# An encoder step on one core: one pool per tile at two changes of stage, the last block and the first up pairs in another order, and a convolution issued behind its own pair's split

## The chip, the core and the metric

One core of a Trainium2 chip runs the whole program. Its engines are TensorE (PE, matrix products), VectorE (DVE), ScalarE (ACT), GpSimd (POOL), and SyncE (SP), which issues most DMAs. Each takes its own instructions in a fixed order; they meet at semaphores. The time is device microseconds of one execution.

## The reference

The kernel computes one layer of a streaming encoder on 1024 prompt tokens and 8 x 16 sample tokens, 1152 tokens in all, with D_MODEL = 1024 and D_FF = 3072:

```
h = rmsnorm(x, g_pre_mix)
qa, ka, va, qb, kb, vb, ga, gb = split(h @ w_in)
oa = band_attention(qa, ka, va, window of 2 chunks, sinks)   # 8 heads, 2 kv heads
ob = band_attention(qb, kb, vb, band of 8 chunks)            # 8 heads
merged = sigmoid(ga) * (oa @ w_oa) + sigmoid(gb) * (ob @ w_ob)
x = x + rmsnorm(merged @ w_out, g_post_mix)
u, g = split(rmsnorm(x, g_pre_ffn) @ w_upg)
c = conv_b + sum over 3 taps of conv_w[tap] * shifted u
y = x + rmsnorm((gelu(c) * g) @ w_down, g_post_ffn)
```

All inputs and outputs are float32; new keys, values and convolution rows are outputs too.

## The kernel before, in words

A float32 product is made of three matrix products: each operand is split into a high part (a cast on ScalarE) and a low part (operand minus high part, on VectorE or GpSimd), and high x high, high x low and low x high are summed in PSUM. So each weight or activation tile costs a ScalarE and a VectorE instruction ahead of its matmuls. The large products (the projections, up, down) use seven block products in place of eight; their sums of blocks are further VectorE work.

The stages are: the projections; **attention** (units 0 to 7, each with sub-bands 0 to 3: scores `s` on PE, bias and maximum on VectorE, exponentials `p` at L701 on ScalarE, reciprocal and normalisation at L714 and L718 on VectorE, transpositions `pt` at L735 on PE, copies `pk` at L737 and L739, values `o`, store to `o_dr` at L753); into its gaps the dense columns of the gates are laid (`d`, L117 to L119, evicted as `gt` at L570); **merge** (L920 to L1000): `outputs` loads the eight attention outputs oT0 to oT7 (L931), casts (L932) and subtracts (L933); class `Rows` makes a row block of 128 of merged^T: `start` loads the gate and takes its sigmoid (L945), `part` multiplies (mp, L956 to L958), `gated` multiplies by the gate and so empties PSUM (mm, L962), `merge` adds the two branches (L967) and splits the sum into mT; **third** (L1015 to L1120): wt0 to wt7, the tiles of w_out, are loaded and split (`split_w`, L101 and L104); for each of nine blocks of 128 tokens the row product r (L1090 to L1092), Square (L1098), norm and residual (L1100, L1101), second norm (L1105), and a transposition `tp` (L1074) into the four quarters bq (L1080), from which the right factors b11, b21, t3, ... of the up stage are split; **up** (L1126 to L1300): 24 tiles f of the hidden width, each with u and gate; **down** (L1309 on).

In the up stage the first five tiles (NH = 5) have two of their products made ahead (`head_away`): xh<f> from b11, stored to a_dr, and after b21 is added, stored to c_dr. Later `head_back` and `up_rows` load these again (`a`, and `w`, the row buffer). For each f `tail` then makes the products with t3, t2, t1, b22, t4, and `take` (L1200) adds the product x and the loaded a on VectorE, which also frees the PSUM banks of x. `conv` works on the rows w: one tap on ScalarE (L1239), two on VectorE (L1241), then GELU.

Order: a scheduler lays every engine's instructions in a fixed order by priorities that come from the order of the code, and by costs that it assumes. `issue_after(i)` keeps instructions behind i, `high_priority(offset)` moves them ahead. Tiles live in pools of SBUF or PSUM space; a pool opened where an earlier one was closed waits until the instructions that used that space are done (by tile, with reuse_waits="tile"). In the kernel before, the eight oT tiles lie in one pool (op), and the eight wt tiles in one pool (wp3).

## Time and profile before

| what | value |
|---|---|
| time, median of 3 runs | 1635.86 us (1635.2 to 1637.76) |
| the profiled execution | 1635.94 us, its span 1634.1 us |
| PE busy | 1593.4 us, 98% of the span |
| VectorE busy | 1099.4 us, 67% |
| ScalarE busy | 728.7 us, 45% |
| GpSimd busy | 212.1 us, 13% |
| chain that ended last | PE 86%, DVE 5%, ACT 3%, DMA 3% |

How to read it: the busy share of PE counts a matmul that runs at the lower level of the clock with its longer time, so a stretch can be full and slow at once. The granted clock of the whole execution is 0.994. The idle time in front of an instruction is given in brackets, with the instruction that ended it.

### The profile page before, as it was taken

What the parts mean: (1) busy time and instruction counts of PE and PEld (TensorE: products, weight loads), DVE (VectorE), ACT (ScalarE), POOL (GpSimd) and SP (SyncE); (2) the same over time, 40 slices, a digit from 0 to 9 for tenths busy, and PEclk for the clock granted to TensorE, in tenths of its full rate; (3) what the DMA queues carried; (4) which work ended last, traced back from release to release, by engine and by line L of the source; (5) the groups of instructions that cost most, each with busy time, mean ns of one, the idle gap of its engine ahead of it and who ended that gap; (6) DMA issues with size and microseconds to landing.
All of it is one profiled execution on the core that took longest, in us unless ns stands there. A gap on an engine that the chain in (4) does not pass through costs nothing.

```text
span 1634.1 us, 27922 instructions
## 1 busy us (share of the span) xinstructions
PE 1593.4 (98%) x10891; PEld 1470.7 (90%) x10891; DVE 1099.4 (67%) x2045; ACT 728.7 (45%) x1429; POOL 212.1 (13%) x287
## 2 busy tenths in 40 slices
PE   8999999999999999999999999999999999999998
PEld 6999999878788889978899999999999998888886
DVE  6976544777676746444497866766666767955997
ACT  7521233566555444332374344444444445434252
POOL 1000000221110004410002212211112211000002
PEclk9999999999999999999999999999999999999999
DMA  7654321654443255342264321221221219053023
GB/s 282 205 183 150 111 103 67 222 174 152 152 157 102 67 184 195 119 161 90 78 189 136 117 80 57 82 81 67 82 69 67 81 49 367 1 204 124 1 78 154
DMA packets 93045, 205.94 MB, mean 126 GB/s; under 512 B 19321, under 2 KB 42793, under 8 KB 92914
## 3 DMA queue, kind: packets, MB, share of 16 engines
q1 hardware_dynamic: 92640, 203.35, 36.2%
q8 instruction: 85, 1.39, 0.4%
q0 software_dynamic: 272, 0.81, 0.1%
q14 instruction: 46, 0.38, 0.1%
q10 hardware_dynamic: 2, 0.00, 0.0%
HBM read 147.61 MB, written 61.24 MB: 128 GB/s over the span
## 4 chain that ended last, share of the span: by engine, by line
PE 86%; DVE 5%; ACT 3%; DMA 3%; issue 2%; POOL 1%; SPq 0%; DVEq 0%; POOLq 0%; ACTq 0%
PE x L143 16%; PE z L143 8%; PE x L1415 8%; PE ix L143 7%; PE p L1415 6%; PE iz L143 4%; PE y L143 4%; PE o L750 2%; PE d L117 2%; PE pt L735 2%; PE d L119 2%; PE r L1090 2%; PE mp L956 2%; PE mp L958 2%; PE mp L957 2%; PE d L118 2%
## 5 line engine op out<-in xcount | busy, mean ns | idle before, releaser
L143 PE MATMUL x<-xot,s 128*128 128x288 f32 x1152 | 157.7, 295 | 1.5 <-DVE w L1200 1.5
L143 PEld LDWEIGHTS x<-xot,s 128*128 128x128 f32 x1152 | 154.9, 188 | 1.7 <-ACT a L1049 1.7
L1415 PE MATMUL x<-wbp,zap 128*128 128x512 f32 x576 | 135.3, 389 | 0.0
L1415 PEld LDWEIGHTS x<-wbp,zap 128*128 128x128 f32 x576 | 108.1, 188 | 22.5
L1049 ACT ACTIVATE s<-uw 128x512 fp32r<-128x512 f32 x96 | 60.2, 627 | 94.8 <-issue 41.7
L1415 PE MATMUL p<-wbp,zap 128*128 128x512 f32 x432 | 100.5, 389 | 0.0
L701 ACT ACTIVATE p<-p,m 128x256 f32<-128x256 f32 (+4 forms) x128 | 74.8, 587 | 57.3 <-DVE m L696 57.2
L1415 PEld LDWEIGHTS p<-wbp,zap 128*128 128x128 f32 x432 | 81.1, 188 | 16.9
L1050 DVE TENSOR_TENSOR s<-uw,s 128x512 fp32r<-128x512 f32 x96 | 70.2, 731 | 33.8 <-ACT s L1049 33.7
L1241 DVE SCALAR_TENSOR_TENSOR wk<-w,cw,wk 128x128 f32<-128x128 f32 (+2 forms) x144 | 83.2, 614 | 6.7 <-ACT wk L1239 5.9
L1050 DVE TENSOR_TENSOR a<-uw,a 128x512 fp32r<-128x512 f32 x62 | 42.9, 693 | 63.4 <-ACT a L1049 62.2
L143 PE MATMUL x<-xob,s 128*128 128x288 f32 x576 | 81.1, 295 | 3.3 <-DVE wk L1200 3.3
L143 PEld LDWEIGHTS x<-xob,s 128*128 128x128 f32 x576 | 78.1, 188 | 3.9 <-ACT wk L1239 3.1
L143 PE MATMUL z<-xot,s 128*128 128x288 f32 x576 | 80.7, 295 | 0.0
L143 PE MATMUL z<-xot,a 128*128 128x288 f32 x576 | 80.7, 295 | 0.0
L143 PE MATMUL ix<-t,s_i 128*128 128x256 f32 (+1 forms) x576 | 78.4, 294 | 0.7 <-DVE iu L191 0.7
L143 PEld LDWEIGHTS z<-xot,s 128*128 128x128 f32 x576 | 78.1, 188 | 0.0
L143 PEld LDWEIGHTS z<-xot,a 128*128 128x128 f32 x576 | 78.1, 188 | 0.0
L143 PEld LDWEIGHTS ix<-t,s_i 128*128 128x128 f32 x576 | 76.8, 187 | 0.9 <-DVE iu L191 0.9
L176 ACT ACTIVATE s_i<-iw 128x512 fp32r<-128x512 f32 x48 | 30.1, 631 | 86.2 <-PE ix L143 38.1
L143 PE MATMUL x<-xob,a 128*128 128x288 f32 x456 | 63.9, 295 | 0.0
L143 PE MATMUL y<-xob,a 128*128 128x288 f32 x456 | 63.9, 295 | 0.0
(634 smaller groups left out, 3837.1 us busy)
## 6 DMA issues: line engine op xcount, KB each, us to landing
uw<-in_w_upg SPq DMA_DIRECT2D x53, 512.0 KB, 3.7
iw<-in_w_in SPq DMA_DIRECT2D x24, 512.0 KB, 3.7
gg<-in_dr SPq DMA_DIRECT2D x16, 576.0 KB, 4.1
z_dr<-wk SPq DMA_DIRECT2D x23, 256.0 KB, 2.1
in_dr<-gt SPq DMA_DIRECT2D x30, 192.0 KB, 1.9
z_dr<-wk SPq DMA_DIRECT2D x23, 224.0 KB, 1.9
xt<-in_x SPq DMA_DIRECT2D x9, 512.0 KB, 7.6
oT<-o_dr SPq DMA_DIRECT2D x8, 576.0 KB, 6.5
```

The costliest lines, as they stand in the source:

```text
L117: nc.tensor.matmul(ps, w[:, 0, a], xg[0][:, b], start=start and k == 0, stop=False)
L118: nc.tensor.matmul(ps, w[:, 0, a], xg[1][:, b], start=False, stop=False)
L119: nc.tensor.matmul(ps, w[:, 1, a], xg[0][:, b], start=False, stop=stop and k == nk - 1)
L143: nc.tensor.matmul(ps, w[:, i, k], right(j, c, k), start=first and n == 0, stop=last and n == len(todo) - 1, skip_group_check=True)
L701: nc.scalar.activation(p[h][:, 0:n], p[h][:, 0:n], AF.Exp, bias=least[h], scale=-1.0, accum_out=st.d[:, h, i:i + 1])
L735: nc.tensor.transpose(pt[:, h * nb + b], st.p[i][h][:, c:c + P], ident[:])
L750: nc.tensor.matmul(ps[r, c], k.vs[:, kb, r], p[h], start=n == 0, stop=n == len(st.pv) - 1)
L956: nc.tensor.matmul(ps[:], self.sp[:, 0, k], oT[k][:, 0, c], start=k % 4 == 0, stop=False)
L1049: nc.scalar.activation(sp[:, 0], src, AF.Copy)
L1050: nc.vector.tensor_tensor(sp[:, 1], src, fr(sp[:, 0]), op=ALU.subtract)
L1241: nc.vector.scalar_tensor_tensor(out, src(t), cw[:, f, t:t + 1], out, op0=ALU.mult, op1=ALU.add)
L1415: nc.tensor.matmul(ps, z[:, i, k, c], w[:, j, k], start=first and n == 0, stop=last and n == 2, skip_group_check=True)
```

## The change

- **End of attention.** The last dense pieces come from one stream, four, then the transpositions, two, then the values, then the rest. The last eviction gt moves from ScalarE to VectorE, and the tile vs has a pool of its own.
- **Merge.** Eight pools in place of one for oT. The load and splits of oT2 to oT7, of the second row's weights and of the gates are issued behind the cast of oT1. The parts k come in pairs.
- **Third.** A pool per wt tile, the row buffers placed behind the fourth; the splits of wt have a higher priority (200).
- **Last block.** The transpositions of the two blocks before the last stand within the last block's product (k = 1 and 6). The last block's own normed rows lie in the unused end of two bq tiles, in two halves, and are transposed in the up stage.
- **Up.** Two weight tiles of the away pairs share a load buffer; three single pools for the split left factors, by turns. `Away` in place of `head_away`: the pairs 0, 1, 2 go by turns, first the b11 products of all three, then the last block's transpositions, then the b21 products; then pairs 3 and 4. `conv(0)` of these five pairs is issued behind the cast of the split that was made last, which is the pair's own s1; the right factors still to be made (`form`) are issued behind the last away split.

```diff
-        run(pieces[0])
+        rest = stream(pieces)
+        for _ in zip(range(4), rest):
+            pass
         for _ in transposes(prev):
             pass
-        run(pieces[1])
+        for _ in zip(range(2), rest):
+            pass
         values(prev)
-        run(*pieces[2:])
+        for _ in rest:
+            pass
...
-        op = ph.enter_context(tc.tile_pool(name="op", bufs=1, reuse_waits="tile"))
+        op = [ph.enter_context(tc.tile_pool(name=f"op{u}", bufs=1, reuse_waits="tile")) for u in range(8)]
...
-        oT = [op.tile([P, 2, T], F32R, name=f"oT{u}") for u in range(8)]
+        oT = [op[u].tile([P, 2, T], F32R, name=f"oT{u}") for u in range(8)]
...
-                nc.scalar.activation(oT[u][:, 0], raw, AF.Copy)
+                cast = nc.scalar.activation(oT[u][:, 0], raw, AF.Copy)
                 nc.vector.tensor_tensor(oT[u][:, 1], raw, fr(oT[u][:, 0]), op=ALU.subtract)
+            return cast
 
...
-        first = [Rows(n) for n in range(2)]
-        outputs(range(4))
-        for r in first:
-            r.start(0)
-        outputs(range(4, 8))
-        for k in range(4):
+        first = [Rows(0)]
+        cast = outputs(range(2))
+        with tc.issue_after(cast.ins):
+            first.append(Rows(1))
+            outputs(range(2, 4))
+            for r in first:
+                r.start(0)
+            outputs(range(4, 8))
+        for k in range(0, 4, 2):
             for r in first:
                 for g in groups:
-                    r.part(0, g, k)
+                    for i in range(2):
+                        r.part(0, g, k + i)
...
-        xp = ph.enter_context(tc.tile_pool(name="xp3", bufs=2, reuse_waits="tile"))
-        gp = ph.enter_context(tc.tile_pool(name="gp3", bufs=1, reuse_waits="tile"))
-        gpm = bcast_row(gp, g_post_mix, D, "gpm")
-        gpf = bcast_row(gp, g_pre_ffn, D, "gpf")
-        gp.tile([P, 768], F32, name="gap")
-        wp = ph.enter_context(tc.tile_pool(name="wp3", bufs=1, reuse_waits="tile"))
-        wo = [wp.tile([P, 2, D], F32R, name=f"wt{k}") for k in reversed(range(KD))][::-1]
+
+        wo = []
+        for k in range(KD):
+            wp = ph.enter_context(tc.tile_pool(name=f"wp3{k}", bufs=1, reuse_waits="tile"))
+            wo.append(wp.tile([P, 2, D], F32R, name=f"wt{k}"))
+            if k == 3:
+                xp = ph.enter_context(tc.tile_pool(name="xp3", bufs=2, reuse_waits="tile"))
+                gp = ph.enter_context(tc.tile_pool(name="gp3", bufs=1, reuse_waits="tile"))
+                gpm = bcast_row(gp, g_post_mix, D, "gpm")
+                gpf = bcast_row(gp, g_pre_ffn, D, "gpf")
         for k in range(KD):
             raw = (wr if k % 4 > 1 else wr2).tile([P, D], F32, name=f"wt{k}r", tag="wr")
             nc.sync.dma_start(raw[:], w_out[k])
-            split_w(raw, wo[k], "scalar", "vector")
+            with tc.high_priority(offset=200):
+                split_w(raw, wo[k], "scalar", "vector")
...
+        wop = [left_pool(i) for i in range(2)]
...
+        last_rows = []
...
+            t = r1[2 * h + q].tile([P, 4 * 3 * 256], F32, name=f"bq{h}{q}", tag="act")
+            bq[h][q] = t[:, 0:8 * CW].rearrange("p (c k n) -> p c k n", c=2, k=4)
+            if not h:
+                last_rows.append(t[:, 8 * CW:8 * CW + 512])
...
+        def away_weights(f):
+
+            if f not in uraws:
+                raw = raw_weights(range(f, min(f + 2, NH)))
+                uraws.update({f: raw[:, 0], f + 1: raw[:, 1]})
+            return uraws.pop(f)
...
+            sp = wop[next(turn) % 3].tile([P, 2, 4, P], F32R, name=name, tag="wop")
+            split["left"] = nc.scalar.activation(sp[:, 0], src, AF.Copy)
+            split["low"] = nc.vector.tensor_tensor(sp[:, 1], src, fr(sp[:, 0]), op=ALU.subtract)
...
+        def transpose_block(halves, tb, pool):
             for q in range(2):
-                pt = pst.tile([P, 4, P], F32, name=f"tp{tb}_{q}", tag="pt")
+                pt = pool.tile([P, 512], F32, name=f"tp{tb}_{q}", tag="ps")[:].rearrange("p (k n) -> p k n", k=4)
                 for k in range(4):
-                    nc.tensor.transpose(pt[:, k], src[:, (4 * q + k) * P:(4 * q + k + 1) * P], ident[:])
+                    nc.tensor.transpose(pt[:, k], halves[q][:, k * P:(k + 1) * P], ident[:])
...
+                if i == 8 and k in (1, 6):
+                    transpose_block(*pending.pop(0), pst)
...
+            halves = [h2[:, q * 512:(q + 1) * 512] for q in range(2)]
+            rows = halves if i < NT - 1 else last_rows
+            for q in range(2):
+                qs = slice(q * 512, (q + 1) * 512)
+                nc.vector.scalar_tensor_tensor(rows[q], xt[:, qs], st[:, 3:4], gpf[:, qs], op0=ALU.mult, op1=ALU.mult)
+            pending.append((rows, tb))
+            while 3 <= i < 8 and len(pending) > 2:
+                transpose_block(*pending.pop(0), pst)
             if i == 6:
                 for c in range(2):
                     split_chunk("b11", bq[0][0], c, nc.vector)
-                early_op[0] = split_left(uraws[0][:, 0, 0:4], "h11_0")
-        for p in pending:
-            transpose_block(*p)
+                for f in range(2):
+                    early_op[f, 0] = split_left(early_raw[f][:, 0:4], f"h10_{f}")
+        (last_block,) = pending
...
+        class Away:
+
+
+            def __init__(self, f, pool):
+                self.f, self.raw = f, early_raw[f] if f in early_raw else away_weights(f)
+                self.xb = banks(pool, f"xh{f}")
+
+            def run(self, i):
+                f = self.f
+                left = early_op.pop((f, i), None) or split_left(self.raw[:, 4 * i:4 * i + 4], f"h1{i}_{f}")
+                product(self.xb, left, of(("b11", "b21")[i]), i == 0, i == 1)
+                out = [pa.tile([P, CW], F32, name=f"{'ac'[i]}h{f}_{c}", tag="a") for c in range(2)]
+                snap(self.xb, [t[:] for t in out])
+                for c in range(2):
+                    nc.sync.dma_start((a_dr, c_dr)[i][f][:, c], out[c][:])
...
-            c1 = conv(0)
+            if yb is None:
+                with tc.issue_after(split["left"].ins):
+                    c1 = conv(0)
+            else:
+                c1 = conv(0)
...
+        def away(*pools, block=None):
+
+            some = [Away(f, pool) for f, pool in pools]
+            for i in range(2):
+                for e in some:
+                    e.run(i)
+                if block and not i:
+                    transpose_block(*block, psz)
+
+        def form():
+
+            with tc.issue_after(ahead[0].ins), tc.issue_after(ahead[1].ins):
+                next(forms, None)
+
+        early_raw[2] = away_weights(2)
+        early_op[2, 0] = split_left(early_raw[2][:, 0:4], "h10_2")
         forms = right_factors()
         next(forms)
-        for f in range(NH):
-            head_away(f)
-            if f in (1, 2):
-                next(forms)
+        away((0, psx), (1, psx), (2, psz), block=last_block)
+        ahead = split["left"], split["low"]
+        form()
+        away((3, psx), (4, psx))
+        form()
```

**ScalarE in attention, around the four exponentials of unit 6, sub-band 2** (p6_2_..., with sums dn6_2; pcs6 belongs to the samples, pk are copies of transposed p, gt an evicted dense column, oms6 the samples' values). Before:

```order
L809 ACTIVATE pcs6_6549<-ts6_6544 128x512
L701 ACTIVATE p6_2_0_0_6522,dn6_2_6521<-p6_2_0_0_6522,m6_2_6520 128x640
L701 ACTIVATE p6_2_0_1_6523,dn6_2_6521<-p6_2_0_1_6523,m6_2_6520 128x640
L701 ACTIVATE p6_2_1_0_6558,dn6_2_6521<-p6_2_1_0_6558,m6_2_6520 128x640
L701 ACTIVATE p6_2_1_1_6559,dn6_2_6521<-p6_2_1_1_6559,m6_2_6520 128x640
L570 ACTIVATE gt32_1_6603<-d32_1_6551 128x384
L824 ACTIVATE oms6_6617<-os6_6606 128x256
```

After:

```order
L813 ACTIVATE pcs6_6552<-ts6_6547 128x512
L705 ACTIVATE p6_2_0_0_6525,dn6_2_6524<-p6_2_0_0_6525,m6_2_6523 128x640
L705 ACTIVATE p6_2_0_1_6526,dn6_2_6524<-p6_2_0_1_6526,m6_2_6523 128x640
L940 ACTIVATE oT0_7484<-oT0_7484 128x1152
L705 ACTIVATE p6_2_1_0_6561,dn6_2_6524<-p6_2_1_0_6561,m6_2_6523 128x640
L705 ACTIVATE p6_2_1_1_6562,dn6_2_6524<-p6_2_1_1_6562,m6_2_6523 128x640
L574 ACTIVATE gt32_1_6606<-d32_1_6554 128x384
L828 ACTIVATE oms6_6620<-os6_6609 128x256
```

The cast of oT0 (L940) stands between the second and the third exponential, where there was no work of the merge.

**VectorE at the end of the merge** (mm7_g_b is row 7's product for column group g and branch b, out of PSUM mp7_g_b; wt0 to wt7 are the low parts of w_out). Before:

```order
L962 TENSOR_TENSOR mm7_1_0_8312<-mp7_1_0_8299,gg7_0_8266 128x384
L962 TENSOR_TENSOR mm7_2_1_8330<-mp7_2_1_8317,gg7_1_8314 128x384
L967 TENSOR_TENSOR mm7_2_0_8282<-mm7_2_0_8282,mm7_2_1_8330 128x384
L962 TENSOR_TENSOR mm7_0_1_8348<-mp7_0_1_8335,gg7_1_8314 128x384
L967 TENSOR_TENSOR mm7_0_0_8297<-mm7_0_0_8297,mm7_0_1_8348 128x384
L962 TENSOR_TENSOR mm7_1_1_8366<-mp7_1_1_8353,gg7_1_8314 128x384
L967 TENSOR_TENSOR mm7_1_0_8312<-mm7_1_0_8312,mm7_1_1_8366 128x384
L104 TENSOR_TENSOR wt0_8402<-wt0r_8403,wt0_8402 128x1024
L104 TENSOR_TENSOR wt1_8401<-wt1r_8407,wt1_8401 128x1024
L104 TENSOR_TENSOR wt2_8400<-wt2r_8411,wt2_8400 128x1024
L104 TENSOR_TENSOR wt3_8399<-wt3r_8415,wt3_8399 128x1024
```

After:

```order
L971 TENSOR_TENSOR mm7_1_0_8337<-mp7_1_0_8324,gg7_0_8291 128x384
L104 TENSOR_TENSOR wt0_8416<-wt0r_8455,wt0_8416 128x1024
L104 TENSOR_TENSOR wt1_8420<-wt1r_8459,wt1_8420 128x1024
L104 TENSOR_TENSOR wt2_8424<-wt2r_8463,wt2_8424 128x1024
L104 TENSOR_TENSOR wt3_8428<-wt3r_8467,wt3_8428 128x1024
L971 TENSOR_TENSOR mm7_2_1_8355<-mp7_2_1_8342,gg7_1_8339 128x384
L971 TENSOR_TENSOR mm7_0_1_8373<-mp7_0_1_8360,gg7_1_8339 128x384
L976 TENSOR_TENSOR mm7_2_0_8307<-mm7_2_0_8307,mm7_2_1_8355 128x384
L976 TENSOR_TENSOR mm7_0_0_8322<-mm7_0_0_8322,mm7_0_1_8373 128x384
L971 TENSOR_TENSOR mm7_1_1_8391<-mp7_1_1_8378,gg7_1_8339 128x384
```

The subtractions of wt0 to wt3 moved from behind the last multiply and addition to a place ahead of the three multiplies with branch 1.

**VectorE in the up stage, pair f = 1** (s1_1, a22_1 are left factors of pair 1, x1, z1 its products in PSUM, w1 and w2 the row buffers of pairs 1 and 2, uw its weights, wk the working tile). Before:

```order
L1050 TENSOR_TENSOR s4_1_9906<-uw12_9795,s4_1_9906 128x512
L1200 TENSOR_TENSOR w1_9660<-x1_0_9798,a1_0_9791 128x288
L1200 TENSOR_TENSOR w1_9660<-x1_1_9799,a1_1_9792 128x288
L1050 TENSOR_TENSOR a22_1_9939<-uw12_9795,a22_1_9939 128x512
L1241 SCALAR_TENSOR_TENSOR wk_9701<-w2_9858,cw_9220,wk_9701 128x448
L1200 TENSOR_TENSOR wk_9701<-x1_0_9798,a1_0_9791 128x288
L1241 SCALAR_TENSOR_TENSOR wk_9701<-w2_9858,cw_9220,wk_9701 128x448
L1228 TENSOR_TENSOR w1_9660<-z1_0_9800,wk_9701 128x288
L1200 TENSOR_TENSOR wk_9701<-x1_1_9799,a1_1_9792 128x288
L1241 SCALAR_TENSOR_TENSOR wk_9701<-w2_9858,cw_9220,wk_9701 128x128
```

After:

```order
L1084 TENSOR_TENSOR s2_1_9900<-uw1_9864,s2_1_9900 128x512
L1084 TENSOR_TENSOR s1_1_9935<-uw1_9864,s1_1_9935 128x512
L1284 SCALAR_TENSOR_TENSOR wk_9770<-w1_9729,cw_9281,wk_9770 128x448
L1284 SCALAR_TENSOR_TENSOR wk_9770<-w1_9729,cw_9281,wk_9770 128x128
L1284 SCALAR_TENSOR_TENSOR wk_9770<-w1_9729,cw_9281,wk_9770 128x448
L1243 TENSOR_TENSOR w1_9729<-x1_0_9867,a1_0_9860 128x288
L1284 SCALAR_TENSOR_TENSOR wk_9770<-w1_9729,cw_9281,wk_9770 128x128
L1084 TENSOR_TENSOR s4_1_9975<-uw1_9864,s4_1_9975 128x512
L127 TENSOR_TENSOR uw2_10049<-uw2_10049 128x512
L1243 TENSOR_TENSOR w1_9729<-x1_1_9868,a1_1_9861 128x288
L1084 TENSOR_TENSOR a22_1_10008<-uw1_9864,a22_1_10008 128x512
L1243 TENSOR_TENSOR wk_9770<-x1_0_9867,a1_0_9860 128x288
```

Before, rows of the convolution of w2 (L1241) stand ahead of the takes that read x1 into wk (L1200). After, the convolution of pair 1 itself stands right behind s1_1, and none of w2 is ahead of these takes (L1243).

On PE the order behind the last block changes too: before, the last r, transpositions of block 6, xh0, xh0 with b21, the last transpositions; after, the last r (with the transpositions of the two blocks before it inside), xh0, xh1, xh2 from b11, the last block's transpositions, then the three from b21.

## Rows read from the trace of the kernel before

**Rows 1.** The page: busy time and instructions of each engine, and one row of the DMA issues (KB each, median us from issue to landing).
```profile
PE 1593.4 (98%) x10891; PEld 1470.7 (90%) x10891; DVE 1099.4 (67%) x2045; ACT 728.7 (45%) x1429; POOL 212.1 (13%) x287
...
gg<-in_dr SPq DMA_DIRECT2D x16, 576.0 KB, 4.1
```

**Rows 2.** What PE waited for over the whole span: us in total, times, longest us.
```profile
PE x L143 <- DVE wk L1200: 3.3, 3, 1.4
...
PE x L143 <- DVE w L1200: 1.5, 1, 1.5
...
PE tp L1074 <- ACT bq L1080: 1.0, 1, 1.0
...
PE tp L1074 <- DVE h L1105: 0.3, 1, 0.3
```

**Rows 3.** Three stretches of 4 us: at the start of the merge, at the start of the third stage, and at its end. Columns: length, busy us and instructions of PE, PEld, DVE, ACT, POOL, then the granted clock of PE, the share of the DMA engines, GB/s.
```profile
604.00:608.00 4.00, 4.00 (x16) 4.00 (x15) 2.72 (x2) 2.87 (x3) 0.00 (x0) 0.58 1.03 420
708.00:712.00 4.00, 4.00 (x11) 2.99 (x10) 3.60 (x4) 2.29 (x3) 0.00 (x0) 0.50 0.63 199
820.00:824.00 4.00, 2.05 (x15) 1.81 (x14) 3.56 (x6) 3.31 (x7) 0.93 (x1) 1.00 0.54 205
```

**Rows 4.** PE's timeline at the start of the merge: start, us, engine, line, operation, out<-in, count, and in brackets the idle time before it and what ended it.
```profile
601.18 1.33 PE L956 MATMUL mp<-oT,wo0s 128*128 128x384 f32 x3 [2.62 <-ACT oT L932]
...
606.79 0.52 PE L958 MATMUL mp<-oT,wo1s 128*128 128x384 f32 x1
607.11 0.44 PE L956 MATMUL mp<-oT,wo0s 128*128 128x384 f32 x1
607.38 0.34 PE L957 MATMUL mp<-oT,wo0s 128*128 128x384 f32 x1
607.56 0.34 PE L958 MATMUL mp<-oT,wo0s 128*128 128x384 f32 x1
```

**Rows 5.** The tile oT: its casts (duration in ns, shortest, median, longest; first and last start), and its loads.
```profile
L932 ACT ACTIVATE oT<-oT x8: 1152/1165/1168, 600.0 to 614.8; 128x1152 fp32r<-128x1152 f32 x8
...
DMA to landing us min/median/max: 3.9/6.5/10.5
```

**Rows 6.** The timeline of SP: the store of an attention output during unit 6, and the first loads of oT.
```profile
523.36 0.32 SPq L753 DMA_DIRECT2D o_dr<-oo  x1
...
595.06 0.92 SPq L931 DMA_DIRECT2D oT<-o_dr  x2
```

**Rows 7.** PE's timeline at the start of the third stage.
```profile
706.99 0.80 PE L1090 MATMUL r<-wt,mT2h 128*128 128x512 f32 x1 [2.77 <-ACT wt L101]
...
712.70 0.59 PE L1092 MATMUL r<-wt,mT2l 128*128 128x512 f32 x1
713.13 0.40 PE L1090 MATMUL r<-wt,mT2h 128*128 128x512 f32 x1
713.37 0.39 PE L1091 MATMUL r<-wt,mT2h 128*128 128x512 f32 x1
```

**Rows 8.** ScalarE's timeline there: the last sigmoid of the merge, and the first two casts of w_out.
```profile
696.17 1.17 ACT L945 ACTIVATE gg<-gg 128x1152 f32<-128x1152 f32 x1 [2.62 <-DMA gg<-in_dr]
...
705.89 1.04 ACT L101 ACTIVATE wt<-wt0r 128x1024 fp32r<-128x1024 f32 x1
706.84 1.04 ACT L101 ACTIVATE wt<-wt1r 128x1024 fp32r<-128x1024 f32 x1
```

**Rows 9.** VectorE's timeline there: the last multiply out of mp, the first two subtractions of w_out.
```profile
704.25 0.56 DVE L962 TENSOR_TENSOR mm<-mp,gg 128x384 f32<-128x384 f32 x1 [0.87 <-PE mp L958]
...
706.97 1.23 DVE L104 TENSOR_TENSOR wt<-wt0r,wt 128x1024 fp32r<-128x1024 f32 x1 [1.54 <-ACT wt L101]
708.11 1.22 DVE L104 TENSOR_TENSOR wt<-wt1r,wt 128x1024 fp32r<-128x1024 f32 x1
```

**Rows 10.** PE's timeline from the end of the third stage on, and one of the away pairs.
```profile
814.36 1.04 PE L1074 MATMUL tp<-ident,h 128*128 128x128 f32 x8
...
822.71 2.40 PE L143 MATMUL xh<-xob,h 128*128 128x288 f32 x16 [1.95 <-ACT h L1049]
...
882.32 3.43 PE L143 MATMUL x<-xob,s 128*128 128x288 f32 x24 [1.43 <-DVE wk L1200]
```

**Rows 11.** ScalarE's timeline in that pair: the first tap of the next pair's convolution.
```profile
880.33 0.76 ACT L1239 ACTIVATE wk<-w,cb,cw 128x448 f32<-128x448 f32 x1 [1.90 <-DMA w<-c_dr]
```

**Rows 12.** VectorE's timeline: the first multiply of the last block's norm, and in that pair a tap of the convolution and a take.
```profile
816.67 1.28 DVE L1100 SCALAR_TENSOR_TENSOR h<-r,str,gpm 128x1024 f32<-128x1024 f32 x1 [0.73 <-POOL str L97]
...
881.12 0.68 DVE L1241 SCALAR_TENSOR_TENSOR wk<-w,cw,wk 128x448 f32<-128x448 f32 x1 [1.97 <-ACT wk L1239]
881.73 0.45 DVE L1200 TENSOR_TENSOR wk<-x,a 128x288 f32<-128x288 f32 x1
```

**Rows 13.** ScalarE's timeline in attention: the third of the four exponentials of p6_2, and a copy near the end of the last unit.
```profile
527.84 0.83 ACT L701 ACTIVATE p<-p,m 128x640 f32<-128x640 f32 x1 [1.06 <-DVE m L696]
...
587.08 0.60 ACT L739 ACTIVATE pk<-pt 128x512 f32<-128x512 f32 x1 [0.81 <-PE pt L735]
```

**Rows 14.** VectorE's timeline in attention: the reciprocal behind these exponentials, and the normalisation.
```profile
529.61 0.18 DVE L714 RECIPROCAL dn<-dn 128x4 f32<-128x4 f32 x1 [1.33 <-ACT p L701]
529.82 1.94 DVE L718 TENSOR_SCALAR p<-p,dn 128x640 f32<-128x640 f32 x4
```

**Rows 15.** PE's timeline in attention: the transpositions of the normalised p6_2.
```profile
532.02 1.09 PE L735 MATMUL pt<-ident,p 128*128 128x128 f32 x8
```

57 lines of the change are left out of this document (22 added, 35 removed).

## The prediction

> **What bounds the kernel now.** I read the page's busy shares first: TensorE (PE) is busy 1593.4 of 1634.1 us [rows 1]. The change leaves its 10891 matmuls as they are, so all that can be won is idle time of PE and time in which it runs slowly. [...] The timelines then give each place. Three boundaries and one loop matter here: attention to merge [rows 4], merge to third stage [rows 7], third to up stage [rows 10], and the five up pairs whose first products were put away. From the first of the waits for L1200 to the end PE waits for nothing but these takes, so the later reorderings are priced at nothing: their cover is PE's own queue of work.
>
> The profiled execution took 1635.94 us, 1.84 more than its span and 0.08 more than the median (1635.86). The sum is made against 1635.94; a measurement of this kernel can tell about 0.2% (3.3 us) from no change.
>
> **Attention to merge: 5.4 us won.** Before, one pool holds all eight oT tiles, so the first load is issued when the last reader of the attention's space is done, at 595.06 [rows 6]. PE has idled 2.62 us when mp starts at 601.18, released by the cast of L932, and runs at the low level until 607.11 [rows 4]; the stretch from 604 shows a clock of 0.58 [rows 3]. These 5.93 us hold 18 matmuls of 384 columns, 0.32 us apart, where later ones follow at 0.17 to 0.18: 18 x 0.155 = 2.8 lost. With eight pools each oT tile waits only for what stood in its own space. SP then issues oT0 behind the store of 523.36 [rows 6], and oT1 to oT3 during the last unit, a good 15 us ahead of the merge. Casts and subtractions go into idle time of ScalarE, which is 45% busy over the span [rows 1]. oT5 to oT7 are loaded late, but b = 0 (k = 0 to 3) of two rows is 72 matmuls, 12 us of cover. Gain 2.62 + 2.8 = 5.4; at least 2.6, if the clock falls for another reason.
>
> **The price in attention: 1.2 us lost.** The cast of oT0 now stands on ScalarE between the second and the third of p6_2's four exponentials. Queued behind it are two exponentials, behind these the reciprocal (529.61 [rows 14]) and the transposition pt that PE takes up at 532.02 [rows 15] with nothing to spare: the normalisation ends some 0.25 us ahead. The third exponential starts at 527.84 [rows 13]. The load is issued about 523.7. The trace has oT landing in 3.9, 6.5 and 10.5 us (shortest, median, longest [rows 5]), the longer ones in pairs behind each other; alone it is nearest to the shortest, and I take the 4.1 of the gg loads of the same size [rows 1]. Then the cast (1.17) ends at 528.95, 1.1 late, and PE idles 1.1 - 0.25 = 0.85. With 3.9 it is 0.65, with 6.5 it is 3.25. oT4's cast stands likewise ahead of the last copy but one of the last unit; before, ScalarE idles 0.81 ahead of the copy of 587.08 [rows 13], which takes most of 1.17: 0.3. Sum 1.2, between 0.3 and 4.
>
> [...] The trace's own durations stand in the sum.
>
> **Merge to third stage: 3.7 us won.** Before, the casts of wt0 to wt3 come behind the last mT cast (705.89 [rows 8]), and r waits 2.77 for the first; then 14 matmuls go 0.43 apart until 713.13, later 0.24 or less [rows 7], and the stretch shows 0.50 [rows 3]: 14 x 0.205 = 2.9 lost. Now ScalarE casts them right after the last sigmoid (696.17 + 1.17 = 697.34 [rows 8]), one each 0.95, done by 701.2. VectorE subtracts wt0 to wt3 (1.14 apart, the four from 698.7 to 703.3) **ahead of** the multiplies that empty mp7 [rows 9]. That is the new wait: two multiplies at 0.56, two additions of tiles of the same size and the last multiply then follow, so it ends at about 703.3 + 5 x 0.56 = 706.1. PE is through at 704.2 (706.99 - 2.77). In the changed kernel the first r takes a PSUM bank pair of which the last mp7 holds one, so PE idles about 2.0 (1.9 and a release) where it idled 2.77: 0.75 won. Whether the clock then holds is not certain: it holds after 1.95 [rows 3, 10] and falls after 2.62 and 2.77 [rows 4, 7]. 2.0 is nearest to 1.95, so I take the whole 2.9: 3.7 together. If it falls, 0.75. The other casts (wt4 to wt7) have some 4 us of r's matmuls as cover.
>
> **End of the third stage: 1.2 us won.** Before, 1.0 (tp <- bq), 1.95 (xh <- h) and 0.3 us (tp <- h) are idle [rows 2, 10]. The last block's transpositions now come between the two rounds of the away products, with three pairs in a round, so all three waits go: 3.2 us. A new one comes. PE's order is now the end of the last r, 12 matmuls of xh0_0 (1.7 us, by the 3.43 for 24 of the row of 882.32), then xh0_1 in the second bank of that r. The bank is free when the norm's first multiply has read it; that one waits for ScalarE's Square, and it goes from 816.67 to 817.95 [rows 12], 2.3 to 3.6 behind the end of r at 814.36 [rows 10]. PE stands there at 814.36 + 1.7 = 816.0. Idle 2.0, again of the size that kept the clock. 3.2 - 2.0 = 1.2. The last transpositions need the same rows after a further multiply chain, some 9 us behind the r, and stand 11 us behind it: nothing.
>
> **Up pairs: 4.3 us won.** PE waits 3.3 + 1.5 = 4.8 us for the takes of L1200 in the away pairs [rows 2]. The row of 882.32 (1.43) shows how: VectorE holds the next pair's convolution (881.12), which had waited 1.97 for ScalarE's part, and this 1.90 for the DMA of the next pair's rows w [rows 11, 12]; the take that PE needs stands behind it (881.73). In the changed order the convolution of pair f stands behind pair f's own split s1, and its rows w were asked for a pair earlier. From f = 2 on I place their landing 8 us ahead; for f = 1 the slack is only some 0.5. All 4.8 go, but in the first pair the subtraction for a22 stands behind two takes: about 0.5 is new. 4.3; between 2.5 and 4.8.
>
> **Sum.** 5.4 - 1.2 + 3.7 + 1.2 + 4.3 = 13.4: 1635.94 - 13.4 = 1622.5 us.
>
> **The rivals.**
> (B) The clock falls after one of the two 2.0 us idles that I keep. For it: they lie between 1.95, which held, and 2.62, which didn't. Against: they are nearer the first. Price 2.9: 1625.4 (both: 1628.3).
> (C) The convolution of the next pair still holds VectorE, since it waits for the c_dr loads, which only moved. For it: f = 1 has little slack. Against: a store and a load lie a pair apart. Price 4.3: 1626.8.
> (E) The third stage's change doesn't do what it says: the space of wt0 to wt3 comes free no earlier, or the raw loads land late. For it: the casts before stood last too [rows 8]. Against: their pools now lie apart and the built order has them behind the sigmoid. 1626.2.
> (D) Slower: the two casts in attention wait for late oT loads. If oT0 and oT4 land after 10.5 us [rows 5], ScalarE stands in front of p6_2's exponentials and of the last copies: idle 7.3 and 6.6 on PE, and at either the clock falls as it does at 601 (2.8 to 2.9). That is 19.7 instead of 1.2: 13.4 + 1.2 - 19.7 = -5.1, 1641.0 us. It decides from a landing of about 8 us in both. For it: the median of 6.5 is not far. Against: the long landings belong to loads issued two at a time among gg loads; here each goes alone.
> [...]
>
> **How the numbers follow.** The forecast 0.60, B 0.17, C 0.10, E 0.05, D 0.05; 0.03 stays for several losses that together end within 0.2%. The range goes from 1619.0 (no loss in attention, clock kept, 2 us less idle at the boundaries than priced) to 1628.5 (both clocks fall, or C with a longer landing). Faster by over 0.2%: 0.60 + 0.17 + 0.10 + 0.05 = 0.92; within 0.03; slower 0.05.
>
> **What would show it.** After the change mp should start without an idle of its own and with a granted clock of 1.00; r should idle about 2 us, released by a VectorE multiply of mp (mm), not by ScalarE's wt, and go on at 0.23; xh should idle about 2 us, released by the norm's multiply; the waits for the takes (3.3 and 1.5) should be gone; a wait pt <- DVE p of 0.6 to 1 us should appear near 532. I am wrong on the clock if r's first matmuls are 0.43 apart, on the loads if oT0 lands in over 6 us, and on the up pairs if VectorE still shows a wait for ScalarE ahead of a take.

## The result and the profile after

The changed kernel took 1624.57 us (median of 4 runs, 1623.97 to 1625.44), the kernel before beside it 1635.53 (1631.14 to 1637.76): ratio 0.9949 [0.9934, 0.9964] (here and below the ratio is to the kernel before measured beside the run, with its 95% interval). Forecast were 1622.5 and a range of 1619.0 to 1628.5. The profiled execution took 1624.30, its span 1622.5, at a mean clock of 0.998. Matmuls are the same in number; PE is busy 6.7 us less than in [rows 1], 6.2 of it between the first mp and the first xh, where the mean granted clock was 0.97 and is now 1.00: most of it is time at the lower clock that has gone.

The page of the changed kernel, busy time and instructions:
```profile
PE 1586.7 (98%) x10891; PEld 1465.6 (90%) x10891; DVE 1104.8 (68%) x2055; ACT 726.9 (45%) x1428; POOL 213.5 (13%) x287
```

What PE waited for in the changed kernel (us in total, times, longest), against [rows 2]:
```profile
PE pt L739 <- ACT pk L743: 5.5, 8, 2.3
...
PE xh L143 <- DVE h L1137: 1.9, 1, 1.9
PE x L143 <- DVE s L1084: 1.6, 1, 1.6
...
PE r L1127 <- DVE mm L971: 1.4, 1, 1.4
...
PE x L143 <- DVE w L1243: 1.1, 2, 0.6
...
PE z L143 <- DVE a L1084: 0.6, 1, 0.6
...
PE x L143 <- DVE wk L1243: 0.3, 1, 0.3
```
The takes of 3.3 and 1.5 have shrunk to 0.3 and 1.1, but two new rows stand beside them: `x <- s` (1.6) and `z <- a` (0.6). The copies `pk` cost 5.5 in 8 waits; before they cost 2.7 in 6.

PE's timeline of the changed kernel at the places of [rows 4, 7, 10, 15]:
```profile
529.52 1.23 PE L739 MATMUL pt<-ident,p 128*128 128x128 f32 x7 [0.34 <-DVE p L722]
...
584.85 0.66 PE L739 MATMUL pt<-ident,p 128*128 128x128 f32 x4 [0.51 <-ACT pk L743]
...
589.12 0.44 PE L739 MATMUL pt<-ident,p 128*128 128x128 f32 x2 [2.31 <-ACT pk L743]
...
599.24 0.34 PE L119 MATMUL d<-xk,w33s 128*128 128x384 f32 x1
599.41 0.34 PE L965 MATMUL mp<-oT,wo0s 128*128 128x384 f32 x1
...
700.86 0.47 PE L1127 MATMUL r<-wt,mT2h 128*128 128x512 f32 x1 [1.45 <-DVE mm L971]
701.17 0.39 PE L1128 MATMUL r<-wt,mT2h 128*128 128x512 f32 x1
...
810.73 5.45 PE L143 MATMUL xh<-xob,h 128*128 128x288 f32 x39 [1.90 <-DVE h L1137]
...
864.99 6.40 PE L143 MATMUL x<-xot,s 128*128 128x288 f32 x46 [1.63 <-DVE s L1084]
```
The merge (mp, 599.41) follows the dense columns without a gap and at 0.17 to 0.18 a matmul. r waits 1.45, where about 2 was forecast, for the multiply mm, and goes on at 0.23. Both are as forecast in kind, and so is the wait of 1.90 at xh. At 589.12 stands a wait that was not priced at that size.

ScalarE's timeline of the changed kernel in the last attention unit shows where it comes from:
```profile
582.76 1.17 ACT L940 ACTIVATE oT<-oT 128x1152 fp32r<-128x1152 f32 x1 [0.39 <-DMA oT<-o_dr]
...
584.21 0.59 ACT L743 ACTIVATE pk<-pt 128x512 f32<-128x512 f32 x1
587.42 1.16 ACT L940 ACTIVATE oT<-oT 128x1152 fp32r<-128x1152 f32 x1 [2.62 <-DMA oT<-o_dr]
588.49 0.58 ACT L743 ACTIVATE pk<-pt 128x512 f32<-128x512 f32 x1
```
ScalarE stands 2.62 in front of a cast whose load has not landed, and the copy `pk` that PE needs is queued behind it. SP had issued the load of the second cast at 580.47, behind a store of an attention output, 6.95 us before the cast could start:
```profile
580.10 0.32 SPq L757 DMA_DIRECT2D o_dr<-oo  x1
580.47 0.42 SPq L939 DMA_DIRECT2D oT<-o_dr  x1
```

To see which places gave the time, I cut each profiled span at the start of the first instruction of six products: `ix` (here its last group, ix<-xk,s_i, at the end of the projections), `mp` (merge), `r` (third), `xh` (last block and away pairs), `z` (first z with left factors s, in the first up pair), `y` (rest of the up stage, and down). A row's sum is its span; in the first line is what the prediction's terms give for each stretch (change).

| profiled execution | to ix | ix to mp | mp to r | r to xh | xh to z | z to y | y to end |
|---|---|---|---|---|---|---|---|
| forecast change | 0 | -1.4 | -3.55 | -3.9 | -0.2 | -4.3 | 0 |
| before | 289.92 | 311.26 | 105.81 | 110.33 | 36.06 | 88.94 | 691.78 |
| after | 288.48 | 310.93 | 101.45 | 106.23 | 35.00 | 88.36 | 692.05 |
| before_again | 292.24 | 311.43 | 103.43 | 109.63 | 35.82 | 88.81 | 691.74 |
| after_again | 288.58 | 309.47 | 101.44 | 106.32 | 35.02 | 88.48 | 692.09 |
| late4 | 289.18 | 308.50 | 101.44 | 106.34 | 36.51 | 88.99 | 692.04 |
| vs_back | 289.77 | 309.53 | 101.44 | 106.24 | 36.53 | 88.34 | 692.05 |
| one_pool | 287.82 | 308.07 | 101.73 | 108.11 | 36.52 | 87.90 | 692.05 |
| wt_pool | 290.41 | 313.19 | 102.78 | 107.97 | 35.01 | 88.36 | 692.08 |
| ends | 288.39 | 311.89 | 100.75 | 107.50 | 34.22 | 88.54 | 692.01 |
| conv_free | 289.15 | 310.10 | 101.45 | 106.35 | 36.50 | 90.33 | 692.02 |
| only_conv | 289.74 | 311.26 | 104.32 | 109.54 | 35.75 | 86.82 | 691.77 |
| no_mult | 291.10 | 310.11 | 101.44 | 106.35 | 36.52 | 84.83 | 692.05 |
| dve_mult | 290.50 | 308.78 | 101.44 | 106.26 | 36.52 | 86.98 | 692.02 |
| best | 288.55 | 309.62 | 101.45 | 106.28 | 34.23 | 85.86 | 692.01 |

The stretch to ix holds the same matmuls in all kernels, yet it runs from 287.82 to 292.24: one profile pair says nothing about 2 us there. In the kernels that leave the up pairs as the change has them, z to y lies between 87.90 and 88.99, so an edit of the pairs can be read there to about half a microsecond. The up pairs gave 0.58 where 4.3 were forecast; merge and third gave 4.36 and 4.10 where 3.55 and 3.9 were.

### The profile page after: what moved, and what is told of

It reads as the page before. It is cut to its first block, busy times and chain, and to the rows that moved or that the text cites. A ratio compares the mean times of both kernels' runs of the same rounds, so it can differ in the third digit from the quotient of the medians.

```text
span 1622.5 us, 27938 instructions
## 1 busy us (share of the span) xinstructions
PE 1586.7 (98%) x10891; PEld 1465.6 (90%) x10891; DVE 1104.8 (68%) x2055; ACT 726.9 (45%) x1428; POOL 213.5 (13%) x287
## 4 chain that ended last, share of the span: by engine, by line
PE 84%; DVE 6%; ACT 4%; DMA 3%; issue 2%; SPq 0%; POOL 0%; DVEq 0%; POOLq 0%; ACTq 0%
PE x L143 17%; PE z L143 8%; PE x L1479 8%; PE ix L143 7%; PE p L1479 6%; PE iz L143 4%; PE y L143 4%; PE o L754 2%; PE r L1127 2%; PE r L1129 2%; PE r L1128 2%; PE mp L965 2%; PE mp L967 2%; PE mp L966 2%; PE d L117 2%; PE d L119 2%
## 5 line engine op out<-in xcount | busy, mean ns | idle before, releaser
L1284 DVE SCALAR_TENSOR_TENSOR wk<-w,cw,wk 128x448 f32<-128x448 f32 (+1 forms) x144 | 86.2, 635 | 2.1 <-ACT wk L1282 1.2
L1084 DVE TENSOR_TENSOR s<-uw,s 128x512 fp32r<-128x512 f32 x96 | 66.8, 697 | 28.4 <-ACT s L1083 28.1
L739 PE MATMUL pt<-ident,p 128*128 128x128 f32 x360 | 56.9, 282 | 8.4 <-ACT pk L743 5.5
```

What stands on the lines that cost most here:

```text
L739: nc.tensor.transpose(pt[:, h * nb + b], st.p[i][h][:, c:c + P], ident[:])
L1084: split["low"] = nc.vector.tensor_tensor(sp[:, 1], src, fr(sp[:, 0]), op=ALU.subtract)
L1284: nc.vector.scalar_tensor_tensor(out, src(t), cw[:, f, t:t + 1], out, op0=ALU.mult, op1=ALU.add)
```

## The experiments

**conv_free: the changed kernel without the convolution's rule.** Two theories for the missing 3.7 us of the up pairs: the rule does nothing, or it does its work and new waits eat it.
```diff
-            if yb is None:
-                with tc.issue_after(split["left"].ins):
-                    c1 = conv(0)
-            else:
-                c1 = conv(0)
+            c1 = conv(0)
```


> The changed kernel without the rule that puts the convolution of the first five pairs behind the pair's own split; all else stays. Theory as predicted: the rule alone removes the 4.8 us of waits for the takes in the pairs, so without it they come back, and the time rises by about 4 us above the changed kernel. Rival: the waits that are left in the changed kernel (3.7 us) have another cause (VectorE held up by GpSimd's multiplies), the rule is worth little, and the time stays within 1.5 us of it.

Measured: 1628.25 (10 runs, 1624.48 to 1634.17), ratio 0.9966 [0.995, 0.9983]; z to y 90.33, 2.0 more than after. What PE waited for in conv_free:
```profile
PE x L143 <- DVE wk L1243: 3.1, 3, 1.5
...
PE x L143 <- DVE s L1084: 1.6, 1, 1.6
...
PE z L143 <- DVE a L1084: 0.6, 1, 0.6
```
The takes are back at 3.1 (0.3 of it stands in the changed kernel too), and `x <- s` and `z <- a` are there without the rule. So the rule works, and these two waits come from the other edits of the up stage. The two `x <- w` of 0.56 and 0.57 are not there: they come with the rule, as the next run confirms.

**only_conv: the kernel before with that rule alone.** The same `issue_after`, put into the kernel before.

> The kernel before, with nothing changed but the rule that puts the convolution of the first five pairs behind the cast of the split made last. Theory as predicted: 4.3 us faster than before (the four waits for takes go). Rival: new waits of the size seen in the changed kernel (3 to 4 us) take their place: 0 to 1.5 us faster.

Measured: 1631.2 (10 runs, 1628.85 to 1634.63), ratio 0.9982 [0.997, 0.9994]; z to y 86.82, 2.1 less than before. The wait that stays, in only_conv:
```profile
PE x L143 <- DVE w L1201: 2.6, 4, 1.0
```
Of 4.8 us of waits the rule removes 2.2. Two of the four that stay are 0.57 and 0.56, at the pairs where the changed kernel waits 0.56 and 0.57. So the rule is worth 2.0 to 2.1 from either side, half of what was priced: less than the expected 4.3, more than the rival's 0 to 1.5. And only_conv's z to y is 1.5 better than that of the whole change.

**no_mult and dve_mult: what the new waits are.** VectorE's timeline of the changed kernel, ahead of the wait at 864.99:
```profile
861.03 1.69 DVE L131 TENSOR_TENSOR uw<-uw 128x512 f32<-128x512 f32 x1
862.64 1.69 DVE L133 TENSOR_TENSOR uw<-uw 128x512 f32<-128x512 f32 x1
864.25 1.28 DVE L1084 TENSOR_TENSOR s<-uw,s 128x512 fp32r<-128x512 f32 x2
```
GpSimd's timeline there:
```profile
860.58 1.59 POOL L1305 TENSOR_TENSOR wk<-wk,w 128x576 f32<-128x576 f32 x1 [1.47 <-ACT wk L1286]
862.13 1.65 POOL L1311 TENSOR_TENSOR wk<-wk,w 128x576 f32<-128x576 f32 x1
```
Each sum of two SBUF tiles on VectorE begins while GpSimd multiplies, and ends 0.55 behind GpSimd's end (862.72 behind 862.17, 864.33 behind 863.78). The split `s` that releases PE stands behind both. In the next pair the convolution's tap at 879.19 takes 1.58, and the sum at 880.70 takes 1.69, while GpSimd multiplies from 878.71 to 881.84; the take that PE then waits 0.56 for is behind these. Two kernels ask whether that is the cause; the first takes GpSimd's multiplies out of the first five tiles, the second puts them on VectorE:
```diff
-            nc.gpsimd.tensor_tensor(c2, c2, gg[:, 1]...
+            if f >= NH:
+                nc.gpsimd.tensor_tensor(c2, c2, gg[:, 1]...
...
-            nc.gpsimd.tensor_tensor(c2, c2, gg[:, 1]...
+            (nc.gpsimd if f >= NH else nc.vector).tensor_tensor(c2, c2, gg[:, 1]...
```
(and the same for c1).

> The changed kernel without GpSimd's two multiplies by the gate product in the first five tiles of the up stage (so z of these tiles is the GELU alone); everything else is in the same order. Theory of a conflict: VectorE's sums of 0.68 us take 1.69 us when they begin while GpSimd multiplies; without the multiplies they take 0.68 us again, and the waits of 1.63, 0.56 and 0.57 us go: 2 to 3 us faster than the changed kernel. Rival: the order of VectorE's rows alone makes these waits; then they stay, and the time is the same.

> The changed kernel with the two multiplies by the gate product in the first five tiles done by VectorE in place of GpSimd. Theory of a conflict: the 1.69 us sums become 0.68 us, the two multiplies cost VectorE some 0.8 us each, so of the 3.5 us that the run without multiplies won, 1.5 to 3.5 us stay. Rival: VectorE is the bound of these pairs, and 1.6 us more work per pair costs what the conflict cost: no change or up to 2 us slower.

Measured: no_mult 1621.66 (4 runs, 1618.38 to 1624.25), ratio 0.9919 [0.9891, 0.9947]; z to y 84.83, 3.5 less than after. The same sums in no_mult:
```profile
864.45 0.68 DVE L131 TENSOR_TENSOR uw<-uw 128x512 f32<-128x512 f32 x1
865.05 0.68 DVE L133 TENSOR_TENSOR uw<-uw 128x512 f32<-128x512 f32 x1
```
0.68 in place of 1.69, and the waits of 1.63, 0.56 and 0.57 are gone; 0.34 and 0.62 in the first pair stay. These waits are 2.8 of the 3.5; the other 0.8 is busy time of PE (84.64 against 83.87), and why it fell is not shown. dve_mult: 1623.65 (4 runs, 1621.43 to 1625.14), ratio 0.9933 [0.9916, 0.9949]; z to y 86.98: with the work on VectorE 1.4 of the 3.5 are kept, just under the 1.5 expected, and waits stay (two for takes, 1.02 and 0.34, two for splits, 0.3 each, and 0.62 for `z <- a`). The 1.02 is not part of the edit: in best, below, the same edit stands without it, with z to y at 85.86, 2.5 less than after. So GpSimd's multiplies are shown as the cause of 2.8 of the 3.7 us that the five waits of the changed kernel's pairs come to. How they hold VectorE up is not shown; each of the three long sums (861.03, 862.64 and 880.70) ends the same 0.55 behind GpSimd's multiply.

**late4 and vs_back: the casts in attention.** late4 holds the last four oT tiles behind the last copy (`copied["pk"]`); vs_back undoes the pool of vs.
```diff
-            outputs(range(4, 8))
+            with tc.issue_after(copied["pk"].ins):
+                outputs(range(4, 8))
...
-                un.vs = vsp.tile([P, 8, P], F32, name=f"vs{nm}", tag="vs")
+                un.vs = stk.tile([P, 8, P], F32, name=f"vs{nm}", tag="vs", bufs=2)
```


> The changed kernel, with the casts and subtractions of oT4 to oT7 issued behind the last ScalarE copy pk of the attention. Theory: the two idles of 0.51 and 2.31 us ahead of the last transpositions pt come from the casts of oT that stand on ScalarE in front of the copies and wait for their loads; with oT4 behind the copies the 2.31 goes and the 0.51 (which belongs to an earlier cast) stays: 2.0 to 2.6 us faster than the changed kernel. Rival: the copies are late for another reason (the transpositions themselves, or the dense columns), and the idle stays: no change. Either way mp starts without an idle, since oT4 is needed only by the second half of the products.

> The changed kernel with the tile vs back in the pool of the other raw tiles. Theory: the pool of its own is what lets unit 0's keys and queries be split before the last rows of the projections, and what lets oT1 to oT4 be loaded within the last unit; without it the attention begins as before (1 to 1.5 us later), the casts of oT no longer stand ahead of the last copies (their waits of 0.5 to 2.8 us go), and mp may wait for oT again: within 2 us of the changed kernel, either way. Rival: the pool has no part in it, and the order at both places is unchanged in its times.

PE's timeline in the last unit in late4, at the two places of 584.85 and 589.12:
```profile
585.01 0.66 PE L740 MATMUL pt<-ident,p 128*128 128x128 f32 x4 [0.17 <-ACT pk L744]
...
586.54 0.87 PE L740 MATMUL pt<-ident,p 128*128 128x128 f32 x6 [0.35 <-DVE pk L742]
```
2.82 became 0.52, and ix to mp is 308.50, 2.4 less than after. The median moved little: 1624.24 (7 runs, 1621.69 to 1629.51), ratio 0.9942 [0.9924, 0.9959]. Its profile lost 1.5 at the away pairs (36.51 against 35.00), of which more below, and the size of the waits differs between executions of the same attention code: together 0.61 in no_mult, 0.70 in conv_free, 1.06 in after_again (0.68 and 0.38), and over 2.5 in ends and wt_pool. So the 0.52 of late4 fits the theory, but its one profile does not price the edit; that the 2.31 comes from the cast rests on ScalarE's rows above. vs_back has none of them at the end of attention and ix to mp 309.53; 1626.65 (4 runs, 1623.69 to 1628.69), ratio 0.9953 [0.9937, 0.9969]. As whole times both are inconclusive against the change.

**one_pool and wt_pool: the pools per tile undone**, first for oT, then for wt (with it the priority of the splits).
```diff
-        op = [ph.enter_context(tc.tile_pool(name=f"op{u}", bufs=1, reuse_waits="tile")) for u in range(8)]
+        op = ph.enter_context(tc.tile_pool(name="op", bufs=1, reuse_waits="tile"))
...
-            wp = ph.enter_context(tc.tile_pool(name=f"wp3{k}", bufs=1, reuse_waits="tile"))
-            wo.append(wp.tile([P, 2, D], F32R, name=f"wt{k}"))
-            if k == 3:
+            if k == 0:
...
+                wp = ph.enter_context(tc.tile_pool(name="wp3", bufs=1, reuse_waits="tile"))
+                wo = [wp.tile([P, 2, D], F32R, name=f"wt{k}") for k in reversed(range(KD))][::-1]
...
-            with tc.high_priority(offset=200):
-                split_w(raw, wo[k], "scalar", "vector")
+            split_w(raw, wo[k], "scalar", "vector")
```


> The changed kernel with one pool for the eight oT tiles, as before; all else stays. Theory: the first loads are issued behind the attention again, mp idles 2.6 us or more on the cast of oT, and the casts no longer stand in the attention, whose end then has no wait on a copy: from the first of the last unit's waits to the first mp some 56 us as before, against 54.2 to 56.4 in runs of the changed kind. What comes behind depends on the clock: 0 us if it stays at 1.00 after the idle, up to 2.9 us if it falls as before. Together 0 to 5 us slower than the changed kernel. Rival, the predicted price: 5.4 us of gain less 1.2 of loss are undone, 4.2 us slower.

> The changed kernel with the third stage's part undone: one pool for the eight tiles of w_out behind the row buffers, and no higher priority for their splits. Theory as predicted: the casts come behind the last cast of mT again, r idles 2.7 to 2.8 us on ScalarE's wt instead of 1.45, and the clock falls for up to 6 us behind it: 1.3 us plus 1.5 to 2.9 us, together 3 to 4 us slower than the changed kernel. Rival: the earlier space was won by the pools of oT alone; then r still starts as in the changed kernel, and the time is the same.

Measured: one_pool 1629.43 (10 runs, 1624.27 to 1632.3), ratio 0.997 [0.9957, 0.9983]; its profile happens to be its fastest run, with mp's idle of 2.15 and 0.60 back and the clock held. Its median is 4.9 above the change's, near the predicted price of 4.2, but this profile can't show where. r waits for wt in it (0.74, 0.72 and 0.39) and not for mm, so the pools of oT have a part in the third stage too. wt_pool 1627.06 (5 runs, 1625.45 to 1631.55), ratio 0.9965 [0.995, 0.998]. What PE waited for in wt_pool:
```profile
PE r L1126 <- ACT wt L101: 2.8, 1, 2.8
...
PE r L1127 <- DVE wt L104: 0.6, 2, 0.4
```
mp to xh is 210.75 there against 207.68: the pools and the priority of wt are worth 3.07 even where the clock holds, as it did in wt_pool behind that idle:
```profile
706.38:709.38 3.00, 2.71 (x11) 1.92 (x12) 3.00 (x3) 2.79 (x3) 0.07 (x1) 1.00 0.24 49
```

**ends: the two idles that the change leaves.** The casts and subtractions of wt2 and later behind the last mm (`copied["mm"]`); the transpositions of the block before the last behind the last r, where PE runs them ahead of the first xh.
```diff
-                split_w(raw, wo[k], "scalar", "vector")
+                if k < 2:
+                    split_w(raw, wo[k], "scalar", "vector")
+                else:
+                    with tc.issue_after(copied["mm"].ins):
+                        split_w(raw, wo[k], "scalar", "vector")
...
-                if i == 8 and k in (1, 6):
+                if i == 8 and k == 1:
...
+        transpose_block(*pending.pop(0), pst)
```


> The changed kernel with two rows moved: the subtractions of wt2 to wt7 behind the last multiply out of mp, and the transpositions of the block before the last behind the last r instead of inside it. Theory: r waits for that multiply, which stands behind four subtractions; with two fewer ahead of it the idle of 1.45 falls to about 0.7. And xh waits 1.90 for the norm's first multiply; with 0.8 us of transpositions laid into it, 1.1 are left, and the clock stays at 1.00 behind it (the stage from xh to the first z then takes 34 to 35 us, against 36.5 where the clock fell). Together 1.5 us faster than the best execution of the changed kernel, 3 us where its clock fell. Rival: r then waits for wt2, or xh for copies that ScalarE now has ahead of the Square, and the idles stay as large.

Measured: 1624.13 (4 runs, 1623.47 to 1625.13), ratio 0.9939 [0.9924, 0.9954]. What PE waited for in ends:
```profile
PE xh L144 <- DVE h L1142: 1.0, 1, 1.0
...
PE r L1132 <- DVE mm L972: 0.7, 1, 0.7
...
PE r L1133 <- DVE wt L105: 0.5, 1, 0.5
PE r L1132 <- ACT wt L102: 0.2, 1, 0.2
```
The first part fails: r waits 0.7 in place of 1.45, but later subtractions give two waits for wt, and r to xh is 1.27 longer, mp to r 0.70 shorter. The second works: xh waits 1.0 in place of 1.90, xh to z 34.22.

**before_again and after_again: both kernels once more**, for the clock behind an idle.

> The kernel before once more, unchanged, for the clock behind its long idles. Theory: whether the granted clock falls behind an idle of 2.6 to 2.8 us, and for how long, differs from execution to execution; then the stretch from mp to r (105.8 us in the profile shown) and the one from r to xh (110.3) are shorter here by up to 2.9 us each, with the same idles. Rival: the clock falls at both places by the same 6 us each time, and both stretches come back within 0.3 us.

> The changed kernel once more, unchanged. Theory: the clock behind the 1.90 us at xh falls in most executions (it did in six of the eight of this shape so far), so the stretch from xh to the first z takes 36.5 us here and not 35.0; and the wait of the last copies for oT lies between 0.5 and 2.9 us, with the landing of its loads. Rival: the changed kernel keeps its clock there, and only the edits of the other kernels lost it: 35.0.

before_again took 1634.16 (10 runs, 1632.75 to 1637.74), ratio 1.0 [0.9988, 1.0011]. PE's timeline in before_again, the two idles of [rows 4, 7], of the same length to 0.01:
```profile
603.67 0.79 PE L956 MATMUL mp<-oT,wo0s 128*128 128x384 f32 x3 [2.63 <-ACT oT L932]
...
707.10 0.50 PE L1090 MATMUL r<-wt,mT2h 128*128 128x512 f32 x1 [2.77 <-ACT wt L101]
```
Stretches of 3 us behind them in before_again (columns as in [rows 3]):
```profile
603.67:606.67 3.00, 2.84 (x15) 2.52 (x16) 2.69 (x3) 1.94 (x2) 0.00 (x0) 1.00 0.95 370
707.10:710.10 3.00, 2.70 (x7) 1.94 (x8) 3.00 (x3) 2.79 (x3) 0.08 (x1) 0.70 0.26 59
710.10:713.10 3.00, 3.00 (x11) 2.35 (x11) 1.77 (x3) 1.06 (x1) 0.00 (x0) 0.73 0.98 292
```
The first idle cost no clock this time, where [rows 3] showed 0.58. The second cost less than before. after_again took 1624.42 (4 runs, 1623.23 to 1628.36), ratio 0.9945 [0.9927, 0.9962]; the clock held there (1.00) behind xh's idle of 1.91, against what I expected. In other kernels it did not. Stretches behind xh's idle of 1.90 in the changed kernel, then in late4:
```profile
810.73:813.73 3.00, 3.00 (x22) 3.00 (x23) 3.00 (x4) 1.96 (x5) 0.00 (x0) 1.00 0.15 64
```
```profile
809.11:812.11 3.00, 3.00 (x17) 3.00 (x18) 3.00 (x4) 1.96 (x5) 0.00 (x0) 0.72 0.15 64
812.11:815.11 3.00, 3.00 (x19) 3.00 (x19) 2.56 (x5) 1.08 (x3) 0.93 (x1) 0.71 0.57 209
```
The same code at this place with the same idle: 22 matmuls in 3 us, or 17. A value such as 0.72 is a mean. In stretches of 0.5 us the clock behind this idle was 1.00 or 0.50, apart from the stretch in which it changed. In late4:
```profile
809.61:810.11 0.50, 0.50 (x6) 0.50 (x5) 0.50 (x2) 0.17 (x1) 0.00 (x0) 1.00 0.00 0
810.61:811.11 0.50, 0.50 (x4) 0.50 (x4) 0.50 (x2) 0.29 (x1) 0.00 (x0) 0.50 0.00 0
```
PE ran at 1.00 for 1 us behind the idle, then at 0.50 until 813.6.

All profiles share one more such place, in attention: an idle ahead of pt (at 417.90 in before), 2.39 to 2.42 us long in every kernel. In 12 of the 14 profiles the clock fell behind it, in one_pool and dve_mult it held. The second 3 us behind it in before, then in one_pool:
```profile
420.90:423.90 3.00, 3.00 (x19) 2.28 (x18) 1.95 (x8) 1.30 (x5) 0.00 (x0) 0.65 0.76 293
```
```profile
417.66:420.66 3.00, 3.00 (x24) 2.59 (x21) 2.60 (x9) 2.28 (x6) 0.00 (x0) 1.00 0.80 311
```

**best: what helped, together** (late4, the transpositions behind the last r, dve_mult).

> The changed kernel with three edits: casts of oT4 to oT7 behind the last copy of the attention; the transpositions of the block before the last behind the last r; the multiplies of the first five up tiles on VectorE. Theory: their gains add, since they lie in three stages: 1.5 to 2.4 us at the end of attention, 0.8 us of idle at xh and with it 1.5 us where the clock fell there, 1.4 us in the up pairs: 1619 to 1621 us. Rival: the clock falls after an idle of 1.1 us at xh too, or elsewhere, and 1.5 us of this come back: 1621 to 1623 us.

Measured: 1621.22 (4 runs, 1619.80 to 1622.18), ratio 0.9917 [0.9902, 0.9932], the fastest kernel here that does the whole computation. Against the change's own medians (1624.57, 1624.42) it is about 3.3 us less. The median misses the expected 1619 to 1621 by 0.2; the profiled execution, 1619.80, lies inside it and kept its clock behind xh (xh to z 34.23). In the up pairs and the away pairs PE waited in best, among others:
```profile
PE xh L144 <- DVE h L1139: 1.0, 1, 1.0
...
PE z L144 <- DVE a L1086: 0.6, 1, 0.6
...
PE x L144 <- DVE wk L1246: 0.3, 1, 0.3
```

## Why the prediction was right, and where it was not

The direction and the mechanisms of the stage changes were right; two terms were too good in this pair, and the total came out near by luck, because others were too small and because both long idles of the profiled kernel before happened to cost clock in full. The sum of 13.4 came out at 11.6 in the profiled pair. By stretches (forecast, measured gain): up pairs 4.3 and 0.58, ix to mp 1.4 and 0.33, so 4.8 too much; against that merge and third 7.45 and 8.46, xh to z 0.2 and 1.06, the projections 0 and 1.44 by chance, the last stretch 0 and -0.27, 3.0 too little.

- **Up pairs, "All 4.8 go": the step that failed.** The takes of [rows 2] are down to 1.4 (two of 0.56 and 0.57 come with the rule itself), but the convolution's rule is worth only 2.0 to 2.1, and other waits came in their place. And "about 0.5 is new" named one wait rightly (`z <- a`, 0.62, in the first pair) and missed 1.63, 0.56, 0.57 and 0.34. The first three hang on GpSimd's multiplies: no_mult removes them. I had looked at the order on VectorE alone, not at what GpSimd does beside it; the trace of before had the sign, a split of 1.60 at 875.26 where others take 0.68 (its rows stand in the last section). What the 0.34 hangs on was not tried; by VectorE's rows its take stands behind the subtraction of a right factor (xot, 852.19, 1.35 us).
- **Attention, "Sum 1.2, between 0.3 and 4": right as a range, mis-sized in its parts.** p6_2 cost 0.34 where I had 0.85: oT0's cast began 4.4 us after its load was issued, but the transpositions (529.52) start before the last of the four normalisations ends, so their slack was more than the 0.25 I took. The last unit cost 2.82 where I had 0.3: I counted the cast, not its wait for the load. The mechanism I had myself described in D, queued behind a cast that waits, struck there 6.95 us after the issue, near the median landing of [rows 5] and short of the 8 us that D asked for. In executions with the same attention code the last unit cost 0.61 to 2.82 and p6_2 0.53 or less, so the term runs from about 0.6 to 3.3.
- **Attention to merge, "Gain 2.62 + 2.8": right in kind.** The idle is gone, and the granted clock is 1.00 in the first 3 us of mp. But the 2.8 is no constant of the kernel before: it was about 0 in before_again.
- **Merge to third, 3.7: right.** r waits for mm as foreseen, 1.45 in place of 2.0, since VectorE was done earlier. wt_pool shows that the pools and the priority do it; E fell.
- **End of third, 1.2: right, xh idles 1.90 where 2.0 was forecast.** B's condition is not settled by the length of the idle: in the profiles with this idle (1.90) the clock held in three (after, after_again, wt_pool: xh to z 35.0) and fell in six (late4, conv_free, no_mult, dve_mult, vs_back, one_pool: 36.5). Both profiles of the unchanged kernel held; the six that fell have the same code here and another edit elsewhere, so that chance alone decides it is likely, but not shown at this place. The price is 1.5, not 2.9.
- **C** was half right: what it feared (VectorE held) happened, through GpSimd.
- What the new order at the start of attention gave isn't settled. The loss in attention and the 2.62 would make ix to mp some 0.5 longer, and it came out 0.33 shorter; vs_back shortens the stretch further, but the scatter of this stretch is as large: 308.78 to 313.19 in the seven kernels and executions that leave attention as the change has it (after, after_again, wt_pool, ends, conv_free, no_mult, dve_mult). One pair can't size this term.

## What to carry to other kernels

Keep an instruction that waits for a DMA from standing on its engine ahead of work that TensorE needs next, and count its wait, not its own duration: a cast of 1.16 us stood 2.62 for its load here, and PE idled 2.31. When VectorE is near the critical path, look at what GpSimd does in the same microseconds; a sum of two SBUF tiles took 1.69 us here beside a GpSimd multiply, 0.68 without it. Judge an edit of a few us by the stretch that it touches, in several executions: whole times of one kernel here scatter by up to 10 us (conv_free). A price for the clock that is read from one execution is the price of that execution.
